# A third seven-product pair in the ninth up panel of each channel mixer

## The chip, the cores and the metric

The kernel runs on one core of one Trainium2 chip. The metric is the device time of one execution in microseconds (us). The core has five engines with queues of their own: TensorE does matrix products (PE in the profile; PEld is its loading of the stationary operand), VectorE (DVE) and ScalarE (ACT) do element-wise work, GpSimd (POOL) and SyncE (SP) here mostly issue transfers.

## The reference

The function is a decoder trunk of two layers on one sequence of 256 tokens, 2,048 wide, in fp32. Each layer is a mixer (gated linear attention in the first, forgetting attention in the second, both with heads that attend into 256 memory tokens) and then a channel mixer, and this document is about the channel mixer:

```python
def causal_dwconv(u, w, b):
    s_ = u.shape[1]
    up = jnp.pad(u, ((0, 0), (CONV_WIDTH - 1, 0), (0, 0)))
    return w[0] * up[:, 0:s_] + w[1] * up[:, 1:s_ + 1] + w[2] * up[:, 2:s_ + 2] + b

def conv_ffn(h, w_up, conv_w, conv_b, w_down):
    u = causal_dwconv(h @ w_up, conv_w, conv_b)
    a, val = split_cols(u, [FFN_HIDDEN, FFN_HIDDEN])
    return (jax.nn.silu(a) * val) @ w_down
```

`FFN_HIDDEN` is 5,632 and `h` is the normalized residual stream (256 x 2048). So `w_up` is 2,048 x 11,264 and `w_down` 5,632 x 2,048, in each layer.

## The kernel before

**Products in parts.** An fp32 operand is kept as two parts, a high part rounded to the format that TensorE takes (`whi`, written by ScalarE at line 231 or 380) and the low rest (`wlo`, VectorE, line 232 or 381). A product is three matmuls: high x high, low x high, high x low. Activations lie split in SBUF as `bufA` or `bufB` (the name in the profile is `A` or `B`, `mix` where the tile was given out again), one tile for each chunk of 128 channels. The weights come from DRAM (`wp`) and are split on the way.

**Panels.** The up projection is done in eleven panels (j = 0, 4, ..., 40; panel number j // 4, from 0). A panel has four blocks of results, two blocks of 128 tokens by two halves of 512 columns, each in a PSUM bank of its own, and runs over the 16 chunks of the 2,048 input channels. The order in a mixer is: up panels 0 to 4, the first part of the down projection (chunks 0 to 15, as two steps of 1,024 columns), up panels 5 to 7, the second part (chunks 16 to 27), up panels 8 to 10, the last part.

**One chunk, or two at once.** `pair_steps` (line 384) runs a panel. A chunk on its own takes `split_unit` (line 210): a 512 KB load to a tile `raw` (four rooms), one cast and one subtraction of 1,024 columns, and 12 matmuls of 512 columns. Two chunks k and k+1 can be taken together as a two-by-two block product with seven products (p1 to p7, with p2, p3 and p4 going to the banks of the blocks) in place of eight, so with 21 matmuls. That asks for sums and differences of the weights (VectorE, lines 435 to 438, in place in two 512 KB tiles `raw2`, of which there are two rooms, so one pair's), for four splits (`split_more`, line 375: one of 512 and three of 1,024 columns), for four banks more (p1, p5, p7, p6), and for sums and differences of the activations (`usum`, in the down projection `dsum`), which are made once by `input_sums` (line 1431) or `gated` (1415) through `token_sums` (468). `whi` and `wlo` have four rooms each; a pair uses all four. The results in p1, p5, p7 and p6 are added in by `early` (1486 for an up panel, 1334 for the down projection) after a panel's last pair.

**Which chunks are paired.** All up panels take chunks 6 and 7 as a pair (`SEVEN_UP`). Panels 5 and 8, those right after a part of the down projection, also take 11 and 12 (`SEVEN_MORE`, `MORE_IN`). In the down projection the pairs begin at chunks 4, 10, 20 and 34 (`SEVEN_DOWN`), with token sums in the rooms `dsum0` and `dsum1`. `pair_steps` puts a pair starting at chunk k where k chunks have been done; with `ahead` = 2, as in panels 5 and 8, two chunks earlier. The order there is 0, 1, 2, 3, 6-7, 4, 5, 8, 11-12, 9, 10, 13, 14, 15.

**The work beside the matmuls.** The results of a panel are turned on VectorE, moved through DRAM by POOL's queue, and come back 32-wide for the convolution (ScalarE, `tap_of`), two additions, silu and the gate (`gated`). These are put out in small steps: at each chunk `tick` (1465) is given a credit (1.45, or 1.7 in panels 5 and 8; 0 in the two ticks of a pair) and issues waiting steps while the credit is positive. Each step is tied behind the last split that was traced (`issue_after`). Splits, loads and pairs' differences have a higher priority by 300 instructions than the evacuations of banks. The final order on each engine is made by a planner from these priorities and from its own estimate of what is ready.

**Banks.** PSUM has four `acc` banks and four more, `ps_o`, two `ps_s` and `ps_t`. From one panel or down step to the next the two sets change places (`flip`): the blocks of one are in the set that takes p1, p5, p7 and p6 of the next.

Of the kernel before, what the change touches and what calls it, by code (L numbers as in the profile page):

```python
# [34 lines left out]
SEVEN_UP = (6,)  # L35
SEVEN_DOWN = {4: 0, 10: 1, 20: 0, 34: 1}
SEVEN_MORE = 11
MORE_IN = (5, 8)


LEVELS = (64, 16, 4)
# [77 lines left out]
def _layout():  # L119

    where, off = {}, 0
    for key, _, kcs, cols, per in _panels():
        n = sum(c[1] for c in cols)
        units = []
        for u in range(0, len(kcs), per):
            units.append((off, kcs[u : u + per], n))
            off += P * per * n
        where[key] = units
    return where, off
# [17 lines left out]
def _trunk(ctx: ExitStack, tc: tile.TileContext, xt, xtok, memt, wp, wgu, gns, gfin, cnv, par, msk, out):  # L147
    nc = tc.nc
    where, _ = _layout()
# [35 lines left out]
    loads, casts, lows, ends, last_mm, sent = [], [], [], [], [], []  # L185
# [282 lines left out]
    def token_sums(r, dst):  # L468

        t = r.rearrange("p s (b n) -> p (s b) n", b=2)  # L470
        a11, a21, a12, a22 = (t[:, n, :] for n in range(4))
        V.tensor_tensor(a22, a21, a22, ALU.add)
        V.tensor_tensor(a21, a11, a21, ALU.subtract)
        V.tensor_tensor(a11, a22, a11, ALU.subtract)
        V.tensor_tensor(a12, a12, a11, ALU.subtract)
        halves([dst[:, part] for part in range(2)], t)
# [903 lines left out]
    def ffn(l, nx, h, m, ys, zs, landing, then, pool, temps, last=None, spare=None):  # L1380
        with tc.tile_pool(name=f"ffn{l}", bufs=1) as fp:
            def held(name, i):
                return pool.tile([P, 2, 4, P], F32R, name=name, tag=f"{name}{i}")

            up_sums = {k: held("usum", k) for k in (*SEVEN_UP, SEVEN_MORE)}
# [45 lines left out]
            def input_sums(k):  # L1431

                r = fp.tile([P, 2, T], F32, name="cv", tag="cv")
                for s in range(2):
                    V.tensor_tensor(r[:, s, :], h[k + s][:, 0, :].bitcast(F32), h[k + s][:, 1, :].bitcast(F32), ALU.add)
                token_sums(r, up_sums[k])


            def scale(b):
                return nx.col()[:, b : b + 1]  # L1440

            def turn(j, wait):

                count[0] += 1
                slot = count[0] % 2
                y, z = ys[slot], zs[slot]

                def evac(b, a):
                    with tc.high_priority(offset=AHEAD):
                        turned_last[0] = V.transpose(y[:, :, :, b, :], a.rearrange("p (k c i) -> p c k i", c=4, i=32))  # L1450
                    if b:
                        away = far_away(dram, flat(y), T, nc.gpsimd)
                        back = lambda: away(flat(z))
                        steps = [(0.5, lambda s=s, c=c, i=i: tap_of(j, s, c, i, slot)) for n in ((1, 2), (0,))
                                 for s in range(2) for c in range(2) for i in n]
                        steps += [(1.0, lambda: add_tap(1)), (1.0, lambda: add_tap(2)), (0.5, silu),
                                  (1.0, lambda: gated(j, 0)), (0.7, lambda: gated(j, 1))]
                        returns.append((clock[0] + 3, slot, back, [(clock[0] + wait, *step) for step in steps]))

                return evac  # L1460

            waiting, clock, credit = [], [0], [0.0]
            returns, unread, turned_last = [], [0, 0], [None]

            def tick(share):

                clock[0] += 1
                credit[0] = min(credit[0], 0.0) + share
                while returns and returns[0][0] <= clock[0] and not unread[returns[0][1]]:
                    _, slot, back, steps = returns.pop(0)  # L1470
                    back()
                    unread[slot] = 12
                    waiting.extend(steps)
                while waiting and waiting[0][0] <= clock[0] and credit[0] > 0:
                    _, cost, step = waiting.pop(0)
                    credit[0] -= cost
                    step()

            def up_pair(j):

                count[2] += 1
                second = j // 4 in MORE_IN
                turns = [turn(j + 2 * h_, 7 if not h_ and j // 4 + 1 in MORE_IN else 8) for h_ in range(2)]
                u = {}

                def early(bank):
                    u.update({(b, h_): temps(2 * b + h_) for b in range(2) for h_ in range(2)})
                    S.activation(u[0, 1], bank["p1"], AF.Copy)
                    S.activation(u[0, 0], bank["p1"], AF.Copy, scale=scale(0))
                    V.tensor_tensor(u[0, 1], bank["p6"], u[0, 1], ALU.add)  # L1490
                    V.tensor_tensor(u[1, 0], bank["p7"], u[0, 1], ALU.add)
                    V.tensor_tensor(u[0, 1], bank["p5"], u[0, 1], ALU.add)
                    V.tensor_tensor(u[1, 1], bank["p5"], u[1, 0], ALU.add)
                    for b, h_ in ((0, 1), (1, 0), (1, 1)):
                        S.activation(u[b, h_], u[b, h_], AF.Copy, scale=scale(b))

                def late(b, h_, a):
                    with tc.issue_after(turned_last[0].ins) if h_ and not b else nullcontext():
                        V.scalar_tensor_tensor(u[b, h_], a, scale(b), u[b, h_], ALU.mult, ALU.add)
                    turns[h_](b, u[b, h_])  # L1500

                return pair_steps(where["up", l, j], h, {k: up_sums[k] for k in (*SEVEN_UP, SEVEN_MORE)[: 1 + second]},
                                  count[2] % 2, pool, early, late, 2 * second)

            def first(k):
# [3 lines left out]
                    input_sums(SEVEN_MORE)  # L1509
                tick(0)  # L1510

            def drive(steps, share=1.45):
                for k in steps:
                    tick(share if k >= 0 else 0.0)

            def drive_up(j):
                drive(up_pair(j), 1.7 if j // 4 in MORE_IN else 1.45)

            for k in SEVEN_UP:
                input_sums(k)  # L1520
            for k in up_pair(0):
                first(k)
            done = 4
            for p, (lo, hi) in enumerate(PARTS[:-1]):
                while done < hi + 4:
                    drive_up(done)
                    done += 4
                src = [m[c % RING] for c in range(lo, hi)]
                for f in (0, 2):
                    count[2] += 1  # L1530
                    drive(down_pair(l, p, f, src, {c - lo: t for c, t in sums.items() if f}, count[2] % 2, pool,
                                    lambda: (temps(0), temps(1))))
                sums.clear()
            lo, hi = PARTS[-1]
            while done < hi:
                drive_up(done)
                done += 4
# [86 lines left out]
    with tc.tile_pool(name="stash", bufs=1) as st:  # L1624
        vt = st.tile([P, 2, FOX_H * HD], F32, name="fvt")
        turned3 = vt.rearrange("p b t -> p (b t)").rearrange("p (f q k b j) -> p f q k b j", f=3, q=4, k=4, b=2)
        turned3 = [turned3[:, f] for f in range(3)]

        with tc.tile_pool(name="turn1", bufs=1) as tp:
            n2, then = preparing("kv", bufB, tp, dram, turned3, "raw2", nc.gpsimd)  # L1630
            ys = [const.tile([P, 4, 4, 2, 32], F32, name="yu", tag=tag) for tag in ("mk0", "mv0")]
            fixed = [vt.rearrange("p b t -> p (b t)")[:, 2048 + 512 * i : 2560 + 512 * i] for i in range(2)]

            def temps(i):
                return fixed[i] if i < 2 else tp.tile([P, 512], F32, name="temp", tag=f"temp{i}")

            more = []
            for t, tag in ((mk, "mk1"), (mv, "mv1")):
                parked.append(dram.tile([P, 4 * T], F32, name="park" + tag, tag="park" + tag, bufs=1))
                nc.gpsimd.dma_start(parked[-1], t[1].rearrange("p a b -> p (a b)"))  # L1640
                more.append(const.tile([P, 2, 2, T], F32R, name="more" + tag, tag=tag))
            ffn(0, n, bufB, bufA + [t[:, i] for t in more for i in range(2)], ys, turned3, ys, then, tp, temps)
        fox(n2, vt, turned3)
# [9 lines left out]
    with tc.tile_pool(name="store", bufs=1) as op:  # L1653
# [55 lines left out]
        then.begin, then.rooms = begin, None  # L1709
        more = [op.tile([P, 2, T], F32R, name=f"more{i}") for i in range(RING - KC)]  # L1710
        ffn(1, n, bufA, bufB + more, ys, zs, zs, then, op, temps, last, spare)


# [68 lines left out]
```

## Time and profile before

| | |
|---|---|
| median of 3 runs | 2213.76 us (2212.93 to 2215.54) |
| profiled execution | 2213.36 us, span of its instructions 2211.5 us |
| TensorE matmuls (PE) | 2200.9 us busy, 10,323 |
| VectorE (DVE) | 1784.5 us busy |
| ScalarE (ACT) | 1420.5 us busy |
| weight loads on SP's queue | 743 of 512 KB, 4.5 us from issue to landing |
| granted clock of TensorE | 0.998 |

All times within the profile are counted from the first instruction. Busy times are sums of rows; matmuls are pipelined, so that a row's 390 ns overlaps its neighbours, and the pace of the stream is read from the start times or from counts in a window. In lists of groups or timelines a row has the line in the kernel, the engine, the operation, what it writes and reads with shapes, how many there were, and in brackets idle time of the engine just before and what ended it.

### The profile page before, as it was taken

The page shows a single profiled execution, that of the slowest core. Times are in us where ns is not written, and L with a number is a line of the kernel's source. Part 1 is how long each engine was busy: PE and PEld are TensorE (multiplying, and loading weights), DVE is VectorE, ACT ScalarE, POOL GpSimd, SP SyncE. Part 2 cuts the span into 40 slices and gives each one's busy share as a digit, 9 for nine tenths or more (in the row PEclk, how much of TensorE's full clock was granted, in tenths as well). Part 3 has the DMA queues.
Part 4 walks back from the last instruction along what each step waited for, and adds up shares of the span by engine and source line. Part 5 has one row for each costly group of instructions (what it writes and reads, how often), then busy time and mean ns, then how long its engine had stood idle before and what let it go on. Part 6 is the DMA issues. An engine that isn't in the chain of part 4 may idle for free.

```text
span 2211.5 us, 30032 instructions
## 1 busy us (share of the span) xinstructions
PE 2200.9 (100%) x10323; PEld 1854.7 (84%) x10323; DVE 1784.5 (81%) x2640; ACT 1420.5 (64%) x2255; POOL 136.5 (6%) x257
## 2 busy tenths in 40 slices
PE   9999999999999999999999999999999999999998
PEld 7888888888888888888888998888888888888886
DVE  7768977688897878888978669668888788988896
ACT  6655664566787568656865555555788656764874
POOL 0000000001100000001110000000101000100000
PEclk9999999999999999999999999999999999999999
DMA  9767567767677567667677767677777757776674
GB/s 347 252 225 224 190 194 234 253 231 254 229 245 263 186 222 242 224 225 246 226 246 264 231 201 246 222 237 249 222 240 245 241 186 247 236 248 218 223 259 153
DMA packets 165713, 515.41 MB, mean 233 GB/s; under 512 B 20716, under 2 KB 41976, under 8 KB 165560
## 3 DMA queue, kind: packets, MB, share of 16 engines
q1 hardware_dynamic: 148488, 460.99, 62.9%
q0 software_dynamic: 16496, 51.71, 7.6%
q8 instruction: 81, 1.33, 0.2%
q10 hardware_dynamic: 576, 0.79, 0.1%
q14 instruction: 72, 0.59, 0.1%
HBM read 469.62 MB, written 43.79 MB: 232 GB/s over the span
## 4 chain that ended last, share of the span: by engine, by line
PE 99%; DMA 0%; DVE 0%; ACT 0%; SPq 0%; issue 0%; DVEq 0%
PE acc L410 30%; PE acc L336 26%; PE ps_s L410 15%; PE ps_o L410 8%; PE ps_t L410 7%; PE acc L307 3%; PE acc L262 3%; PE acc L366 2%; PE ps_s L336 2%; PE acc L260 1%; PE ps_s L1021 0%; PE ps_o L694 0%; DMA raw<-wp 0%; PE ps_s L694 0%; PE ps_s L1294 0%; PE ps_s L1067 0%
## 5 line engine op out<-in xcount | busy, mean ns | idle before, releaser
L232 DVE TENSOR_TENSOR wlo<-raw,whi 128x1024 fp32r<-128x1024 f32 (+2 forms) x707 | 845.4, 1204 | 236.1 <-ACT whi L231 216.6
L231 ACT ACTIVATE whi<-raw 128x1024 fp32r<-128x1024 f32 (+2 forms) x707 | 736.0, 1049 | 410.0 <-PE acc L336 130.5
L336 PE MATMUL acc<-whi,B 128*128 128x512 f32 (+3 forms) x1248 | 291.8, 370 | 0.0
L380 ACT ACTIVATE whi<-raw 128x1024 fp32r<-128x1024 f32 (+1 forms) x136 | 129.8, 954 | 188.9 <-PE acc L410 73.7
L336 PEld LDWEIGHTS acc<-whi,B 128*128 128x128 f32 x1248 | 226.9, 188 | 28.0
L381 DVE TENSOR_TENSOR wlo<-raw,whi 128x1024 fp32r<-128x1024 f32 (+1 forms) x136 | 147.8, 1089 | 59.6 <-ACT whi L380 56.6
L410 PE MATMUL acc<-whi,mix 128*128 128x512 f32 x764 | 194.7, 390 | 0.0
L410 PE MATMUL acc<-whi,B 128*128 128x512 f32 x750 | 192.6, 389 | 0.0
L410 PEld LDWEIGHTS acc<-whi,mix 128*128 128x128 f32 x764 | 143.5, 188 | 29.7
L410 PEld LDWEIGHTS acc<-whi,B 128*128 128x128 f32 x750 | 140.9, 188 | 29.1
L336 PE MATMUL acc<-wlo,B 128*128 128x512 f32 (+3 forms) x624 | 158.5, 369 | 0.0
L336 PEld LDWEIGHTS acc<-wlo,B 128*128 128x128 f32 x624 | 114.6, 188 | 14.6
L1400 ACT ACTIVATE tap<-fvt,cw 128x256 f32<-128x256 f32 x264 | 123.4, 530 | 1.2 <-DMA fvt<-far 1.1
L1400 ACT ACTIVATE tap<-yzu,cw 128x256 f32<-128x256 f32 x264 | 123.4, 531 | 0.4 <-DMA yzu<-far 0.2
L1407 DVE TENSOR_TENSOR tap<-tap,tap 128x1024 f32<-128x1024 f32 x88 | 107.1, 1217 | 1.1 <-ACT tap L1400 1.0
L410 PE MATMUL acc<-wlo,mix 128*128 128x512 f32 x382 | 107.4, 389 | 0.0
L410 PE MATMUL acc<-wlo,B 128*128 128x512 f32 x375 | 107.1, 390 | 0.0
L410 PE MATMUL ps_s<-whi,mix 128*128 128x512 f32 x386 | 105.9, 390 | 0.0
L410 PE MATMUL ps_s<-whi,B 128*128 128x512 f32 x342 | 93.3, 390 | 0.0
L410 PEld LDWEIGHTS ps_s<-whi,mix 128*128 128x128 f32 x386 | 72.5, 188 | 14.9
L410 PEld LDWEIGHTS acc<-wlo,mix 128*128 128x128 f32 x382 | 71.8, 188 | 14.8
L410 PEld LDWEIGHTS acc<-wlo,B 128*128 128x128 f32 x375 | 70.4, 188 | 14.6
(500 smaller groups left out, 3848.6 us busy)
## 6 DMA issues: line engine op xcount, KB each, us to landing
raw<-wp SPq DMA_DIRECT2D x743, 512.0 KB, 4.5
fvt<-far POOLq DMA_DIRECT2D x100, 128.0 KB, 5.6
raw<-wp SPq DMA_DIRECT2D x32, 384.0 KB, 3.5
far<-yu POOLq DMA_DIRECT2D x22, 512.0 KB, 5.8
far<-yzu POOLq DMA_DIRECT2D x22, 512.0 KB, 5.4
yzu<-far POOLq DMA_DIRECT2D x88, 128.0 KB, 5.3
raw<-wp SPq DMA_DIRECT2D x24, 388.0 KB, 4.2
x<-xtok SPq DMA_DIRECT2D x8, 512.0 KB, 7.2
```

Of the source, the lines that this page charges most:

```text
L231: casts.append(S.activation(hi[:, s], raw[:, s], AF.Copy))
L232: lows.append(V.tensor_tensor(lo[:, s], raw[:, s], hi[:, s].bitcast(F32), ALU.subtract))
L260: mm = TE.matmul(acc[p][c][:, :T], w[:, s], both[:, 0, :], start=False, stop=end and j == 3)
L262: mm = TE.matmul(acc[p][c], w[:, s], both, start=u == j == 0, stop=end and j == 3)
L307: mm = TE.matmul(acc[b][:, :n], src[kcs[j] - base][:, part, b * P : (b + 1) * P], w, start=u == 0 and low == part == j == 0, stop=u == end ...
L336: mm = TE.matmul(acc[b][:, :n], src[kc - base][:, part, b * P : (b + 1) * P], ready[low][:, j * room : j * room + n], start=i == low == pa ...
L366: mm = TE.matmul(acc[b][:, :n], src[kc - base][:, part, b * P : (b + 1) * P], w, start=i == low == part == j == 0, stop=i == end and low = ...
L380: casts.append(S.activation(hi[:, :n], src, AF.Copy))
L381: lows.append(V.tensor_tensor(lo[:, :n], src, hi[:, :n].bitcast(F32), ALU.subtract))
L410: r = TE.matmul(bank[name], x, w, start=name not in begun, stop=last)
L1400: S.activation(by_run(taps[i][:, s, c, i:]), zs[slot][:, :, 2 * c + s], AF.Copy if i else AF.Identity, bias=0.0 if i else w[3], scale=w[2 ...
L1407: V.tensor_tensor(taps[0], taps[0], taps[n][:, :, :, :T], ALU.add)
```

## The change

Panel 8 of each channel mixer takes chunks 3 and 4 as a third pair. The token sums for it are made in panel 6, behind its tenth step, into the room `dsum1`, which the down projection's chunk 10 has used and chunk 34 will use; three credits are taken off there. By the rule of `pair_steps` the order in panel 8 becomes 0, 3-4, 1, 6-7, 2, 5, 8, 11-12, 9, 10, 13, 14, 15.

```diff
+SEVEN_THIRD = 3
+THIRD_IN = 8
...
-                return pair_steps(where["up", l, j], h, {k: up_sums[k] for k in (*SEVEN_UP, SEVEN_MORE)[: 1 + second]},
+                keys = (*SEVEN_UP, SEVEN_MORE, SEVEN_THIRD)[: 1 + second + (j // 4 == THIRD_IN)]
+                return pair_steps(where["up", l, j], h, {k: up_sums[k] for k in keys},
                                   count[2] % 2, pool, early, late, 2 * second)
...
-            def drive(steps, share=1.45):
-                for k in steps:
+            def drive(steps, share=1.45, once=None):
+                for i, k in enumerate(steps):
                     tick(share if k >= 0 else 0.0)
+                    if i == 9 and once is not None:
+                        once()
+
+            def third_sums():
+                up_sums[SEVEN_THIRD] = held("dsum", 1)
+                with tc.issue_after(lows[-1].ins):
+                    input_sums(SEVEN_THIRD)
+                credit[0] -= 3.0
 
             def drive_up(j):
-                drive(up_pair(j), 1.7 if j // 4 in MORE_IN else 1.45)
+                drive(up_pair(j), 1.7 if j // 4 in MORE_IN else 1.45, third_sums if j // 4 == THIRD_IN - 2 else None)
```

## The prediction

> **What bounds the kernel now.** I read the page first: busy times, granted clock, the chain that ended last.
>
> ```profile
> span 2211.5 us, 30032 instructions
> PE 2200.9 (100%) x10323; PEld 1854.7 (84%) x10323; DVE 1784.5 (81%) x2640; ACT 1420.5 (64%) x2255; POOL 136.5 (6%) x257
> PEclk9999999999999999999999999999999999999999
> PE 99%; DMA 0%; DVE 0%; ACT 0%; SPq 0%; issue 0%; DVEq 0%
> ```
>
> TensorE is 99% of the chain, at full clock. Only two things can move the time: fewer matmuls, or a hole in their stream. So the next question is where the stream runs closest to what feeds it. For that I read the busy time by stage, with windows set on the ninth up panel (949.82 to 991.98), the tenth, the 21 us ahead of the ninth, the stretch behind its start, and the second half of the seventh panel; then, for the second mixer, the seventh and the 21 us ahead of the ninth.
>
> ```profile
> 949.82:991.98 42.16, 42.16 (x187) 34.94 (x186) 34.39 (x39) 22.75 (x25) 0.00 (x0) 1.00 0.58 198
> 991.98:1034.82 42.84, 42.84 (x190) 35.50 (x189) 34.17 (x40) 32.10 (x51) 5.50 (x10) 1.00 0.74 240
> 933.00:954.00 21.00, 21.00 (x94) 17.39 (x94) 20.63 (x26) 9.97 (x12) 0.00 (x0) 1.00 0.78 272
> 954.00:964.00 10.00, 10.00 (x46) 8.29 (x45) 8.23 (x10) 6.11 (x7) 0.00 (x0) 1.00 0.36 113
> 822.00:845.00 23.00, 23.00 (x103) 19.08 (x102) 20.95 (x28) 21.79 (x37) 0.00 (x0) 1.00 0.76 250
> ...
> 1860.00:1883.00 23.00, 23.00 (x103) 19.08 (x102) 20.93 (x27) 21.78 (x37) 0.00 (x0) 1.00 0.76 251
> 1971.00:1992.00 21.00, 21.00 (x94) 17.38 (x94) 20.74 (x26) 10.20 (x12) 0.00 (x0) 1.00 0.79 275
> ```
>
> Columns: window and its length, then busy time (and count) of PE, PEld, DVE, ACT and POOL, the clock, the DMA share, GB/s. Panel nine holds 186 weight loads in 42.16 us, panel ten 189 in 42.84: both 0.2267 us for each matmul (the 390 ns of a single row overlap with the next). Neither has a hole. But VectorE is busy 20.63 of the 21 us ahead of panel nine, 20.74 in the second mixer: it is full exactly where the change puts more on it.
>
> **The matmuls removed.** A chunk done alone costs 12 matmuls, two chunks 24; as seven products of three they cost 21. One pair more in panel nine of each of two mixers takes away 3 x 0.2267 = 0.68 us each, 1.36 us in all, 0.06%.
>
> **The order inside panel nine.** Today the order is chunks 0, 1, 2, 3, pair 6-7, then 4, 5, 8, pair 11-12, the rest. The third pair becomes second: 0, pair 3-4, 1, pair 6-7, 2, 5, 8, pair 11-12, then 9, 10, 13, 14, 15. So two pairs stand with a single chunk between them, right at the border to the down projection, whose sums VectorE is then still emptying. Pair 6-7 begins after 12 + 21 + 12 = 45 matmuls instead of 48: at 949.82 + 10.20 = 960.02 instead of 960.70.
>
> **What the pair adds to VectorE.** These are its instructions from the border through pair 6-7:
>
> ```profile
> 944.34 1.29 DVE L494 TENSOR_TENSOR x<-x,fvt 128x512 f32<-128x512 f32 x2
> 945.54 1.22 DVE L232 TENSOR_TENSOR wlo<-raw,whi 128x1024 fp32r<-128x1024 f32 x1
> ...
> 949.68 0.68 DVE L494 TENSOR_TENSOR x<-x,ps_o 128x512 f32<-128x512 f32 x1
> 950.28 0.68 DVE L494 TENSOR_TENSOR x<-x,ps_s 128x512 f32<-128x512 f32 x1
> 950.88 0.69 DVE L494 TENSOR_TENSOR x<-x,fvt 128x512 f32<-128x512 f32 x1
> 951.48 0.68 DVE L494 TENSOR_TENSOR x<-x,ps_t 128x512 f32<-128x512 f32 x1
> 952.08 1.22 DVE L232 TENSOR_TENSOR wlo<-raw,whi 128x1024 fp32r<-128x1024 f32 x1
> 953.21 0.68 DVE L494 TENSOR_TENSOR x<-x,ps_s 128x512 f32<-128x512 f32 x1
> 955.00 0.69 DVE L381 TENSOR_TENSOR wlo<-raw,whi 128x512 fp32r<-128x512 f32 x1 [1.10 <-ACT whi L380]
> 955.72 0.69 DVE L435 TENSOR_TENSOR raw<-raw 128x512 f32<-128x512 f32 x1
> 956.33 1.22 DVE L381 TENSOR_TENSOR wlo<-raw,whi 128x1024 fp32r<-128x1024 f32 x1
> 957.47 0.68 DVE L436 TENSOR_TENSOR raw<-raw,raw 128x512 f32<-128x512 f32 x1
> 958.19 0.69 DVE L437 TENSOR_TENSOR raw<-raw,raw 128x512 f32<-128x512 f32 x1
> 958.91 0.69 DVE L438 TENSOR_TENSOR raw<-raw 128x512 f32<-128x512 f32 x1
> 959.52 1.22 DVE L381 TENSOR_TENSOR wlo<-raw,whi 128x1024 fp32r<-128x1024 f32 x1
> 961.14 1.23 DVE L381 TENSOR_TENSOR wlo<-raw,whi 128x1024 fp32r<-128x1024 f32 x1 [0.40 <-ACT whi L380]
> ```
>
> Start to start, a 1,024-wide low half costs 1.14 us (956.33 to 957.47) and a 512-wide operation 0.60 to 0.72. A pair has three of the first and five of the second: 6.4 to 7.0 us. Ahead of pair 6-7 two single chunks (2.28) make room for it, so VectorE has 4.1 us more to do before that pair is ready. ScalarE gets 1.6 us more (3.5 casts of 1.06 for 2); it is busy 6.11 of the 10 us after 954, so it is not the bound.
>
> Its slack: the last low half of pair 6-7 is done at 961.14 + 1.23 = 962.37. TensorE needs it for the pair's 18th matmul, at 960.70 + 17 x 0.2267 = 964.55. That is 2.18 us of slack now; 0.68 of it goes because the pair starts earlier. Deficit: 4.1 + 0.68 - 2.18 = 2.6 us. The idle times in the rows, 1.10 and 0.40, can take 1.5 of it at best. From this side a hole of 1.1 to 2.6 us for each mixer.
>
> **The room of the raw weights.** Each pair loads two 512 KB tiles into two rooms, and the next pair's second load waits until the last low half of the pair before has read its tile. The rows for the issue and landing of pair 11-12, which waits like this today, and ScalarE's part:
>
> ```profile
> L429 SPq DMA_DIRECT2D raw<-wp x2: 328/328/328, 960.8 to 962.4; - x2
> DMA to landing us min/median/max: 3.2/3.4/3.6
> ```
> ```profile
> 949.84 1.07 ACT L231 ACTIVATE whi<-raw 128x1024 fp32r<-128x1024 f32 x1 [2.33 <-PE ps_t L410]
> 958.27 1.06 ACT L380 ACTIVATE whi<-raw 128x1024 fp32r<-128x1024 f32 x1 [2.19 <-DVE raw L436]
> ```
>
> 962.4 is indeed the end of pair 6-7's low halves. With the third pair, pair 6-7 waits for pair 3-4 in this way. The last low half of pair 3-4 writes over chunk 0's, whose matmuls end at 949.82 + 12 x 0.2267 = 952.54; with 0.25 for the signal and 1.22 of work it ends at 954.0 at the earliest. Then the load, 3.4; ScalarE, 1.06; a low half, 1.14; three differences, 2.0; a low half, 1.22: 962.8. TensorE needs that one for the pair's 12th matmul, at 960.02 + 11 x 0.2267 = 962.5. So 0.3 us is missing even if nothing else stands in the way. But by 953.89 VectorE is without a gap today, and the pair's 6.4 for the 3.4 us of chunks 1 to 3 puts 3.0 more into this row: if the low half waits for all of it, it ends at 956.9 and 3.2 us is missing. Hole by this chain: 0.3 to 3.2.
>
> **The accumulators.** The pair's products p1, p5, p7 and p6 go to the banks which the rows above empty (ps_o, ps_s, ps_s, ps_t, the last done at 953.89). Today they are first written at 960.70; then at 952.54, 954.58, 955.26 and 955.94. Slack is 1.4 us on the tightest (955.26 against 953.89). The 3.0 us more on VectorE can fall ahead of these or ahead of the weights, not wholly on both: 0 to 1.6 us here. The three bounds describe the same 3 us on one engine, so I do not add them: 0 to 3.2, and I take the middle of the second chain, 1.8 us for each mixer, which lies inside the first one's 1.1 to 2.6. If evacuation and load chain do add, 3.2 + 1.6 = 4.8.
>
> **The token sums** move into panel seven: two 256-wide and four 128-wide additions, one ScalarE copy and one low half:
>
> ```profile
> L1435 DVE TENSOR_TENSOR cv<-B x4: 412/419/424, 451.4 to 486.5; 128x256 f32<-128x256 f32 x4
> L472 DVE TENSOR_TENSOR cv<-cv x12: 276/283/291, 453.6 to 2090.3; 128x128 f32<-128x128 f32 x12
> L680 ACT ACTIVATE usum<-cv x4: 616/628/633, 462.4 to 1530.7; 128x512 fp32r<-128x512 f32 x4
> L681 DVE TENSOR_TENSOR usum<-cv,usum x4: 683/689/694, 463.1 to 1532.0; 128x512 fp32r<-128x512 f32 x4
> ```
>
> 2 x 0.42 + 4 x 0.28 + 0.69 = 2.7 us of VectorE and 0.63 of ScalarE, where VectorE has 23 - 20.95 = 2.05 idle (2.07 in the second mixer). The credit of 3.0 taken at the same place holds the convolution work back by two steps. I take nothing on the path; without that cover 0.6 us for each mixer. Counting the steps, the work held back is still behind by two when the down projection ends, so its last step falls on the last chunk before panel nine: the additions move inside the full 21 us, they do not leave it. SP issues the same number of loads of the same size (pair 3-4 as two 512 KB tiles, its rooms free since the down projection's pair); POOL gets nothing. Pair 11-12 begins at 949.82 + 102 x 0.2267 = 972.94 and its rooms come free with pair 6-7's last low half, at about 964 to 966, so 7 to 9 us ahead against 11 now (962.4 to 973.62). The chain above needs 3.4 + 1.06 + 1.14 + 2.0 + 1.22 = 8.8 up to a product that starts 2.5 us into the pair: nothing taken, up to 0.5 us if the later end of both holds.
>
> **Sum.** 2 x (1.8 - 0.68) = +2.2 us. The profiled execution took 2213.36 us, 1.9 around its span of 2211.5, so 2215.6; the median of the runs shown, 2213.76, lies 0.4 higher, so 2216.0. What a measurement can tell from no change here is about 0.2%, 4.4 us.
>
> **The rivals.** (1) No hole: the planner lets the evacuations and differences fall into the idle 1.5 us, and chunk 1 stands in for the rest. Then the full 1.36 us is gained: 2212.4. For it: panel nine has two pairs and no hole today. Against it: 0.3 us missing even in the best chain. 0.20. (2) The hole of 0.3 to 2.8 us, as summed: 2213 to 2218. 0.35. (3) Slower beyond 0.2%: VectorE becomes the bound at the border, late with banks and weights in turn, and gaps add instead of overlapping. The point from which this decides is a hole of 2.9 us for each mixer, as 2 x (2.9 - 0.68) = 4.4; at 4.8 it gives +8.2, 2222. For it: 20.63 of 21 busy and 3.0 us put in. 0.36. (4) The hole is one piece of over 3 us and the clock drops. The start of this kernel shows a slow array:
>
> ```profile
> 1.46 4.21 PE L183 MATMUL ps_o<-B 128*128 128x512 f32 x9 [1.46 <-DVE B L180]
> ```
>
> Nine matmuls of 512 take 4.21 us, some 0.43 each, against 0.2267. Nine at that pace lose 9 x 0.20 = 1.8 us behind each hole: with holes of 4.8, 2222 + 3.6 = 2226. 0.06. [...]
>
> **Chances.** Faster 0.03; same 0.20 + 0.35 = 0.55; slower 0.36 + 0.06 = 0.42. The likeliest single time is that of (2) and its own range is 2213 to 2218; the range with four in five reaches from (1) into (3): 2212 to 2223.
>
> **What would show it.** Step one: 183 matmuls in panel nine. Step two: weight rows of L381 for pair 3-4 near 945 to 956, and evacuations of L494 pushed past 954. Step three: idle time of TensorE between 952 and 964, put down to DVE wlo or a DVE evacuation, 1 to 3 us in each mixer, and panel nine at 41.5 + 1.8 = 43.3 us. I am wrong if panel nine takes 41.5 (rival 1), if its hole exceeds 2.9, or if time comes from another stage, the seventh panel above all.

## The result and the profile after

The changed kernel takes 2223.8 us (median of six runs, 2221.39 to 2225.11) against 2213.49 for the kernel before, a ratio of 1.0046 with a 95% interval of 1.0035 to 1.0057: 10.3 us slower. The profiled execution, 2225.11 us, is the slowest of the six; the mean granted clock is 0.997 in the three slowest and 0.999 in the fastest, so the two slow stretches described below need not occur in every execution. The first lines of the page after:

```profile
span 2223.3 us, 30066 instructions
PE 2205.3 (99%) x10317; PEld 1853.2 (83%) x10317; DVE 1796.1 (81%) x2666; ACT 1423.7 (64%) x2261; POOL 136.6 (6%) x257
PE 96%; DVE 2%; DMA 1%; ACT 1%; issue 0%; SPq 0%; ACTq 0%; DVEq 0%
```

The six matmuls are gone (10,317), and yet TensorE's share of the chain fell from 99% to 96%: some of the chain now runs through VectorE, ScalarE and a load. The windows below hold panel nine of both mixers, and two stretches inside the first (columns as before):

```profile
949.97:997.70 47.73, 44.19 (x184) 34.90 (x183) 38.70 (x46) 24.36 (x27) 0.00 (x0) 0.96 0.50 171
968.10:969.60 1.50, 1.50 (x6) 1.09 (x7) 1.50 (x2) 1.50 (x2) 0.00 (x0) 0.96 0.35 139
969.60:973.00 3.40, 3.40 (x10) 2.70 (x9) 3.40 (x4) 1.75 (x3) 0.00 (x0) 0.52 0.71 212
1994.32:2042.06 47.74, 44.31 (x184) 34.78 (x183) 38.69 (x46) 24.34 (x27) 0.00 (x0) 0.96 0.52 174
```

Panel nine took 42.16 us and now takes 47.73, with three matmuls fewer: two times 5.57 us, 11.1 of the 11.8 by which the span grew. TensorE stands for 3.5 us in it by the busy times, and for 3.4 us from 969.60 on the granted clock is 0.52. Six matmuls of panel nine now run at 946.34 already, ahead of the down projection's last sixteen. The window therefore begins at 949.97, where TensorE has done as many matmuls as before panel nine began at 949.82 in the kernel before; it holds as many as the panel has (183 by the weight loads), and next to nothing was lost ahead of it. The timeline of TensorE has the places where it stood, called holes from here on:

```profile
957.32 0.74 PE L412 MATMUL ps_t<-whi,dsum 128*128 128x512 f32 x2 [1.04 <-ACT whi L382]
963.15 0.72 PE L412 MATMUL acc<-whi,B 128*128 128x512 f32 x2 [0.73 <-ACT whi L382]
968.04 0.73 PE L412 MATMUL ps_t<-whi,usum 128*128 128x512 f32 x2 [1.77 <-ACT whi L382]
```

The first is product p6 of pair 3-4 (`dsum`, in the bank `ps_t`), waiting for the cast of the fourth split. The second is p2 of pair 6-7, waiting for the second cast, the third p6 of pair 6-7, again for the fourth. Taken from one matmul's start to the next, less 0.227, the holes are 1.21, 0.89 and 1.93 us; a further 0.1 goes at the next step behind each. The second mixer has the same three (1.21, 0.80, 1.94). The chain that ended last, between 950.09 and 968.04, says why (start, length, what):

```profile
950.09 0.60 DVE x L496
950.69 0.34 DVE mix L527
951.02 0.60 DVE raw L438
951.62 0.34 DVE mix L527
951.96 1.79 DVE x L496 x3
953.75 0.60 DVE raw L439
...
955.41 0.69 DVE raw L440
...
956.21 1.07 ACT whi L382
...
957.29 1.24 DVE wlo L383
...
958.55 3.38 DMA raw<-wp
...
962.03 1.07 ACT whi L382
...
964.27 1.22 DVE wlo L383
965.49 0.61 DVE raw L439
...
966.12 0.70 DVE raw L440
...
966.93 1.06 ACT whi L382
...
968.04 0.73 PE ps_t L412 x2
```

The differences of pair 3-4 (L438 to L440) stand in VectorE's queue between evacuations of the down projection (L496) and the last of the convolution work (L527). So the fourth cast is late, the first hole. With it the last low half is late (957.29), and only when that is done may the second tile of pair 6-7 be loaded (958.55). The second hole is the wait for its landing, and behind the landing come, one after the other, cast, low half, differences and cast: the third hole. From the end of the fourth cast of pair 3-4 (957.27) to p6 of pair 6-7 (968.04) this chain takes 10.8 us.

### The profile page after: what moved, and what is told of

It reads as the page before. It is cut to its first block, busy times and chain, and to the rows that moved or that the text cites. A ratio compares the mean times of both kernels' runs of the same rounds, so it can differ in the third digit from the quotient of the medians.

```text
span 2223.3 us, 30066 instructions
## 1 busy us (share of the span) xinstructions
PE 2205.3 (99%) x10317; PEld 1853.2 (83%) x10317; DVE 1796.1 (81%) x2666; ACT 1423.7 (64%) x2261; POOL 136.6 (6%) x257
## 4 chain that ended last, share of the span: by engine, by line
PE 96%; DVE 2%; DMA 1%; ACT 1%; issue 0%; SPq 0%; ACTq 0%; DVEq 0%
PE acc L412 28%; PE acc L338 26%; PE ps_s L412 15%; PE ps_o L412 7%; PE ps_t L412 7%; PE acc L309 3%; PE acc L264 3%; PE acc L368 2%; PE ps_s L338 2%; PE acc L262 1%; DMA raw<-wp 1%; DVE wlo L383 0%; PE ps_s L1023 0%; ACT whi L382 0%; DVE x L496 0%
## 5 line engine op out<-in xcount | busy, mean ns | idle before, releaser
L382 ACT ACTIVATE whi<-raw 128x1024 fp32r<-128x1024 f32 (+1 forms) x144 | 137.1, 954 | 211.3 <-PE ps_t L412 70.6
L383 DVE TENSOR_TENSOR wlo<-raw,whi 128x1024 fp32r<-128x1024 f32 (+1 forms) x144 | 156.2, 1088 | 63.6 <-ACT whi L382 60.1
```

The costliest lines, as they stand in the source:

```text
L382: casts.append(S.activation(hi[:, :n], src, AF.Copy))
L383: lows.append(V.tensor_tensor(lo[:, :n], src, hi[:, :n].bitcast(F32), ALU.subtract))
```

## The experiments

Four accounts were open: the token sums and the work held back for them; VectorE's queue at the border to the down projection; the two rooms of the pairs' raw weights; and the clock. In the diffs, minus stands for the changed kernel.

**The sums without the pair.**

```diff
-                keys = (*SEVEN_UP, SEVEN_MORE, SEVEN_THIRD)[: 1 + second + (j // 4 == THIRD_IN)]
+                keys = (*SEVEN_UP, SEVEN_MORE, SEVEN_THIRD)[: 1 + second]
```

> The token sums are made in panel seven and the three credits taken, but panel nine keeps its two pairs, so the sums are not used. Theory (the holes in panel nine are the whole loss): no hole appears, 2213.5 us, within 1 us of before. Rival (the sums and the work held back cost on their own): 0.6 us or more for each mixer, up to 2216.

2213.12 us against 2213.00, ratio 1.0000 (0.9991 to 1.0009). The sums and the work held back cost nothing that shows.

**The credits not taken.**

```diff
-                credit[0] -= 3.0
```

> The changed kernel without the three credits taken at the token sums, so the convolution work is not held back and nothing of it is left for the last two chunks before panel nine (two additions and a gate, some 2.5 us of VectorE there). Theory (VectorE's queue at the border makes the first hole, 1.2 us at p6 of pair 3-4): the first hole goes and the rest shrinks by about the same, 2 x 1.5 us or more off 2223.8, about 2219 to 2221 or less if the slow clock goes too. Rival (only the order of the pairs counts): no change, 2223 to 2224.

2222.1 us against 2213.24, ratio 1.0040 (1.0027 to 1.0054). The first hole went from 1.21 to 1.05 us only, and the third stayed 1.93; the second is 0.79 us in the first mixer and 1.21 in the second. So the convolution work that was moved to the border is not what crowds it; the theory's figure for this run, two times 1.5 us, was not met. The time lies 1.7 us below the changed kernel's. In the profiled run the holes add up to about the same, but one of the two slow stretches (1.6 us) is missing, with the same hole ahead of it: windows of the first and the second mixer behind the third hole.

```profile
966.90:970.40 3.50, 3.50 (x16) 2.75 (x17) 3.50 (x4) 3.16 (x4) 0.00 (x0) 1.00 0.51 183
2009.60:2013.00 3.40, 3.40 (x9) 2.58 (x9) 3.40 (x4) 2.57 (x4) 0.00 (x0) 0.51 0.46 169
```

**Less work on VectorE ahead of panel nine.** Four additions to the residual stream are left out of the second part of the down projection (its second step), so the output lacks them; `some_add` adds nothing.

```diff
         def early(bank):
             t0, t1 = temps()
             S.activation(t0, bank["p1"], AF.Copy)
+            add_to = some_add if (p, f) == (1, 2) else every_add
             add_to(f)(0, t0)
...
-            add_to(f + 1)(1, bank["p5"])
+            every_add(f + 1)(1, bank["p5"])
```

> The changed kernel with four of the additions to the residual stream left out in the second down projection's second step (those of the pair's results p1, p6 and p7), so its output is not the reference's; 2.4 us of VectorE less in the 20 us ahead of panel nine. Theory: the first hole (1.2 us) goes, the load of pair 6-7 is issued 1 us or more earlier, and the third hole falls under the size that sends the clock down: 2214 to 2218. Rival (the hole comes of the chain of waits between the engines, not of the amount of work): still 2221 or more.

2218.83 us against 2213.24, ratio 1.0025 (1.0016 to 1.0034), 0.8 above the range that the theory gave. The first hole is gone in both mixers, so with less work at the border it does not arise; the second shrank to 0.07 and 0.40 us. But the third is unchanged, the only one listed in the first mixer. The fourth cast of pair 3-4, from ScalarE's timeline, and the third hole:

```profile
953.95 1.06 ACT L382 ACTIVATE whi<-raw 128x1024 fp32r<-128x1024 f32 x1 [3.04 <-DVE raw L440]
...
965.55 0.73 PE L412 MATMUL ps_t<-whi,usum 128*128 128x512 f32 x2 [1.77 <-ACT whi L382]
```

That cast ends at 955.01, and p6 of pair 6-7 comes 10.5 us later, against 10.8 in the changed kernel. So the chain from this cast over the room and the load to p6 is nearly as long without the border's work, and the third hole is not the border's.

**Other rooms for pair 3-4.**

```diff
-                    ra, rb = [pool.tile([P, NUNIT], F32, name="raw2", tag="raw2", bufs=2) for _ in range(2)]
+                    ra, rb = [rear.tile([P, NUNIT], F32, name="raw", tag="raw", bufs=4) if k == SEVEN_THIRD else
+                              pool.tile([P, NUNIT], F32, name="raw2", tag="raw2", bufs=2) for _ in range(2)]
```

> The changed kernel, but pair 3-4 loads its weights into two of the four rooms of the single chunks, so that pair 6-7's second load need not wait for pair 3-4's last low half. Theory of the rooms: the first hole of panel nine (1.2 us at p6 of pair 3-4) stays, the second (0.9 us, waiting for the load) goes and the third (1.9 us) with the slow clock behind it shrinks below 1 us: 2 x (1.3 to 2.2 - 0.68) over before, 2214.7 to 2216.5 us. Rival (VectorE alone): its queue is no shorter, the third hole stays above 1.5 us with its slow stretch, 2220 us or more.

2216.73 us against 2213.00, ratio 1.0017 (1.0008 to 1.0026), 0.2 above the theory's range. SP's queue issues both tiles of pair 6-7 at 944, where the changed kernel's second went at 958.55:

```profile
944.11 0.90 SPq L432 DMA_DIRECT2D raw<-wp  x2
```
```profile
957.07 0.74 PE L412 MATMUL ps_t<-whi,dsum 128*128 128x512 f32 x2 [1.04 <-ACT whi L382]
963.71 1.20 PE L412 MATMUL ps_s<-whi,usum 128*128 128x512 f32 x4 [0.18 <-ACT whi L382]
965.16 0.74 PE L412 MATMUL ps_t<-whi,usum 128*128 128x512 f32 x2 [0.25 <-ACT whi L382]
```

As TensorE's timeline shows, the first hole stays, the second is gone, the third is 0.34 + 0.42 us in two pieces, and the clock does not drop (mean granted clock 0.999). The rooms are the second and most of the third hole.

**Both at once.** Again the output lacks those four additions.

> Both single cures at once in the changed kernel: pair 3-4 loads into rooms of the single chunks, and four additions to the residual stream are left out ahead of panel nine (the output is not the reference's). Theory (the holes are the vector queue at the border, and the rooms, and nothing else): no hole over 0.3 us in panel nine, no slow clock, 0.8 to 1.4 us less than before, 2211.9 to 2212.6. Rival (something third keeps TensorE waiting, such as the order of the differences): 2214 or more, as with the rooms alone less the first hole.

2212.67 us against 2213.00, ratio 0.9999 (0.9989 to 1.0008). Holes of some 0.2 us are left, with the steps behind them 0.9 us over both mixers by the starts of the matmuls; 1.36 less 0.9 gives 0.5 below before, and 0.3 was measured, which the interval does not tell from nothing. Border and rooms together account for the holes.

**The low half behind the differences.** In the changed kernel's pair 6-7 the low half at 964.27 ran ahead of the two differences that the fourth cast needs. The edit puts it behind them in all three pairs of panel nine.

```diff
-                w3 = split_more(ra, 1024)
+                w3 = split_more(ra, 1024, ready if SEVEN_THIRD in sums else None)   # low half behind the last difference
```

> The changed kernel with the low half of the third split tied behind the pair's last two differences on VectorE, in panel nine alone. In the changed kernel that low half (1.14 us) ran ahead of them in pair 6-7, and the fourth cast, which p6 waits for, had to wait for both. Theory: the third hole shrinks from 1.93 to about 0.8 us and the clock no longer drops: 2 x (1.1 + 1.5) off 2223.8, 2218.6, or, if p5 then waits for its low half instead, 2221. Rival (the load's landing alone sets the third hole): 2223 or more.

2220.73 us against 2213.00, ratio 1.0034 (1.0021 to 1.0047). TensorE's timeline has

```profile
956.18 0.74 PE L413 MATMUL ps_t<-whi,dsum 128*128 128x512 f32 x2 [0.51 <-ACT whi L382]
962.98 0.73 PE L413 MATMUL acc<-whi,B 128*128 128x512 f32 x2 [1.25 <-ACT whi L382]
966.86 0.73 PE L413 MATMUL ps_t<-whi,usum 128*128 128x512 f32 x2 [1.26 <-ACT whi L382]
```

The first and third hole shrank to 0.67 and 1.42 us (1.17 in the second mixer), so the order on VectorE makes about half of the first hole too. But the second grew to 1.41, because p2 came to its wait earlier and the load landed at 961.76 in place of 961.93; the second mixer has 1.20 there and a fourth hole of 0.59 at p1 of pair 6-7. The holes of both mixers add up to nearly what they did, 8.3 us against 8.8, though no slow stretch is left (mean granted clock 0.999): the 3.1 us gained are about the two slow stretches. So the theory was right in the clock and wrong in the sum of the holes; the landing of the load holds the end of the chain.

**The third hole filled.** Eight more matmuls on the low parts, ahead of p6 of pair 6-7 in panel nine; each adds the small product low x low to p7.

```diff
+                if fill and k == fill[0]:
+                    for _ in range(fill[1]):
+                        mm("p7", st[2][1], w3[1][:, 512:], False)
                 three("p6", st[1], [t[:, 512:] for t in w4], done)
```

> The changed kernel with eight more matmuls of 512 columns between p7 and p6 of pair 6-7 in panel nine, each adding the low x low product to p7 (a term some 2 to the 24th smaller, harmless): 1.81 us of work where TensorE stood for 1.94. If the third hole is what sends the clock down, the eight matmuls at 0.43 us go back to 0.227, 1.6 us for each mixer: 2220.5 us. If the slow clock comes of the other holes or of something else, the time stays at 2223.8; if the matmuls only add, 2227.

2221.07 us against 2213.00, ratio 1.0037 (1.0023 to 1.0050), 2.7 below the changed kernel with 16 matmuls more. No slow stretch is left, and the mean granted clock is 0.999 in all five executions; the window behind p6:

```profile
968.00:971.50 3.50, 3.50 (x17) 2.78 (x16) 3.50 (x4) 2.66 (x4) 0.00 (x0) 1.00 0.53 181
```

Without the hole the clock stays up, 1.00 in this window against 0.52 behind the hole of the changed kernel: the slow stretch is the hole's consequence, and by its eight matmuls at 0.427 in place of 0.227 us it is 1.6 us of each mixer's loss.

**Longer holes.** In the kernel before, the cast of chunk 12 is repeated in eight up panels of each mixer.

```diff
-                casts.append(S.activation(hi[:, s], raw[:, s], AF.Copy))
+                for _ in range(1 + again):
+                    casts.append(S.activation(hi[:, s], raw[:, s], AF.Copy))
```

> The kernel before, with the cast of chunk 12 done over 8 to 12 times more in each up panel but the first, sixth and ninth, so that TensorE stands before that chunk for a length that grows with the count, from none to some 3 us, 16 places in two mixers. It shows the clock behind single holes. [...]

2451.45 us, one run. The holes came out at 9.3 to 15.3 us, far over the none to 3 that were asked for, so this run says nothing about short ones; each of the 16 is followed by 8 to 12 matmuls at 0.43 us. With fewer repetitions:

> As the run with the repeated casts, but 2 to 5 more casts in place of 8 to 12, whose holes came out at 9 to 15 us. By the slope of that run, about 1.5 us for each repetition, the holes should be 0 to 5 us. [...]

2336.96 us, one run. The holes are 2.8 to 7.7 us, again longer than planned. All from 3.87 up are followed by 5 to 13 slow matmuls. The two at the short end, the same place in the two mixers, fell out differently. TensorE's timeline at the first and at the second:

```profile
535.06 0.73 PE L412 MATMUL ps_o<-whi,B 128*128 128x512 f32 x2 [2.61 <-ACT whi L233]
...
1636.16 0.74 PE L412 MATMUL ps_o<-whi,A 128*128 128x512 f32 x2 [2.62 <-ACT whi L233]
```

and the windows behind the second and the first (clock in the third column from the end):

```profile
1636.20:1641.00 4.80, 4.80 (x21) 3.95 (x22) 4.80 (x5) 0.10 (x1) 0.00 (x0) 1.00 0.48 147
...
536.10:539.40 3.30, 3.30 (x9) 2.62 (x8) 3.30 (x4) 0.00 (x0) 0.00 (x0) 0.50 0.60 212
```

**The pairs spread.** Sums and pairs as in the change; the order in panel nine is given by hand.

```diff
+SPREAD = [0, 1, 2, 5, 6, 8, 9, 11, 10, 13, 3, 14, 15]
...
+        plan = order or plan
```

> Same three pairs, same sums, but the order in panel nine is 0, 1, 2, 5, pair 6-7, 8, 9, pair 11-12, 10, 13, pair 3-4, 14, 15: two single chunks between pairs, four ahead of the first. Theory (place next to the border and next to each other makes the holes): no hole, 186 - 3 matmuls, 1.36 us less than before, 2212.1 us. Rival (a third pair is too much for VectorE or for the two rooms wherever it stands): holes of about 1 us or more for each mixer, 2214 us or more.

2211.81 us against 2213.00, ratio 0.9994 (0.9986 to 1.0003). Panel nine has no hole. One of 0.76 us is left 24 us into panel ten of the second mixer (not at its start, as the next expectation says), where ScalarE's queue stood behind a transfer of the convolution's input; another of 0.80 us, at 1163.17, lies outside the channel mixers. ScalarE's row:

```profile
2049.80 1.31 ACT L1404 ACTIVATE tap<-yzu,cw 128x256 f32<-128x256 f32 x3 [3.10 <-DMA yzu<-far]
```

With `SPREAD = [0, 1, 2, 6, 5, 8, 11, 9, 10, 3, 13, 14, 15]`:

> Order in panel nine 0, 1, 2, pair 6-7, 5, 8, pair 11-12, 9, 10, pair 3-4, 13, 14, 15: as in the spread order, but with three single chunks ahead of the first pair and three behind the last, so that the last pair's results are taken up before the panel ends. Theory: the one hole of 0.76 us that the spread order left at the start of panel ten of the second mixer goes, none comes at the border: 1.36 us below before, 2211.6. Rival (three chunks are too few at the border): holes of about 0.5 us or more for each mixer, 2212.6 or more.

2211.75 us against 2213.24, ratio 0.9994 (0.9985 to 1.0003). Panel nine in both mixers:

```profile
949.53:991.01 41.48, 41.48 (x185) 34.37 (x183) 36.83 (x45) 22.24 (x24) 0.00 (x0) 1.00 0.52 180
1986.87:2028.46 41.59, 41.59 (x185) 34.20 (x183) 35.76 (x43) 22.24 (x24) 0.00 (x0) 1.00 0.51 177
```

41.48 us is 183 times 0.2267: no hole, with the three pairs in the panel. The panel is 0.68 and 0.57 us shorter than before, and the median lies lower by 1.2 to 1.5 in the two spread orders; the interval just takes in no change, so the gain is shown by the trace and not by the times.

**A second pair in every other up panel too,** on top of the last order: `second = j > 0`, order 0, 1, 2, 3, 6-7, 4, 5, 8, 9, 11-12, 10, 13, 14, 15, credit 1.7.

> The early spread order in panel nine, and pair 11-12 also in the eight up panels that had one pair, in the order 0, 1, 2, 3, 6-7, 4, 5, 8, 9, 11-12, 10, 13, 14, 15, with a credit of 1.7 in all of them. If spread pairs cost no hole anywhere, 16 more pairs take 16 x 0.68 = 10.9 us off 2211.8: 2201. Rival (VectorE, 34.2 of 42.8 us busy in panel ten, cannot take 4.1 us more beside the convolution, or the evacuations are late at the panels' ends): holes eat the gain, 2208 or more.

2266.14 us against 2213.00, ratio 1.0231 (1.0214 to 1.0248). The rival's forecast held, and far beyond what it gave. Holes of 0.5 to 2.9 us stand at the pairs in most of these panels, and seven slow stretches behind them; TensorE's timeline at one hole:

```profile
556.94 1.20 PE L415 MATMUL ps_s<-whi,usum 128*128 128x512 f32 x4 [1.51 <-ACT whi L384]
```

By the starts of the matmuls, holes of over 0.23 us add up to 48 us (0.4 in the run with the early spread order), the slow stretches to 12 more than there, the steps behind holes to 6 more; less the 10.9 us of matmuls taken away, this is 55 of the 56 us by which the span is longer than that run's. So the loss lies in these holes. What makes each of them late, VectorE beside the convolution, the evacuations or the credit of 1.7, was not traced.

## Why the prediction was wrong

It gave 2216.0 us, 2212 to 2223, and the likeliest case within 0.2%; measured is 2223.8, slower beyond that.

*Matmuls removed, 0.68 us for each mixer:* right. 10,317 are left, and a panel nine without holes takes 41.48 us.

*The order inside the panel:* right, 0, 3-4, 1, 6-7, by the rows. With the same pairs in another order nothing is lost.

*VectorE full at the border; the room of the raw weights:* both mechanisms were at work. The chain of the second, load, cast, low half, differences, ran as written, 3.38 us for the landing against 3.4. But the first was worked out for pair 6-7 alone, and the first hole stands at pair 3-4 itself.

*"The three bounds describe the same 3 us on one engine, so I do not add them":* this is the step that failed. They add, because they bite one after the other. The border delays the fourth cast of pair 3-4, and p6 waits for it, 1.32 us with the step behind it; no term of the sum has this wait. The room's chain then starts from that same cast, and the landing of its load holds up pair 6-7 twice (1.0 and 2.1). That is 4.4 us where I took 1.8: the room's chain measured 3.1, inside its 0.3 to 3.2 but 1.3 above the middle that I took, and the 1.32 is missing altogether. The removal runs show the parts: less work takes out the first hole and leaves the third, other rooms take out the second and most of the third and leave the first, and both together leave 0.9 us over the two mixers.

*The room's chain, 0.3 us at best:* too small. With the border's work taken out, the second and third hole with their steps are still 2.1 us in the first mixer and 2.5 in the second. At best I let the last low half of pair 3-4 end at 954.0, as soon as it had a room to write to; in that run it still had to wait for its own cast, which ends at 955.01, and the load went out at 956.29. The 0.25 for the signal is in the trace before: the low half at 965.27, released by the last matmul on `ps_s`, starts 0.26 us behind the start of the next matmul, at 965.01. And in my chain the last link was the low half for p5; on the chip it was the fourth cast for p6, behind a low half that had been put ahead of the differences.

*The accumulators, 0 to 1.6 us:* no matmul in panel nine of either mixer waited for a bank, so 0: TensorE's waits there, 3.5 and 3.4 us, are all for ScalarE's casts. VectorE's added work went ahead of the weights: the last of the evacuations ends at 953.75, against 953.89 before.

*The clock, as a rival with 0.06 and only with a hole of over 3 us in one piece:* the second part of the failure. No run stood behind the 3 us. It needed no such hole; 1.93 us was followed by the slow stretch in both mixers, eight matmuls x 0.2 = 1.6 us each. Holes and clock give 4.4 + 1.6 - 0.68 = 5.3 us for each mixer, 10.6 in all, against the 11.1 by which the two panels grew in the profiled execution and the 10.3 between the medians.

*The sums at no cost:* right, 2213.12 against 2213.00. *Work held back stays inside the full 21 us:* right; giving it back took 0.16 us off the first hole.

Rival 3, slower with gaps that add, came nearest: +8.2 at holes of 4.8 us, without the clock. Its 4.8 lies near the 4.4 in part by luck: 1.6 of it was for banks, which cost nothing.

## What to carry to other kernels

A stage in which the bound engine never waits can have its slack used up by a change that takes work off that engine; ask of each helper's chain how much it is ahead, and when the wait for one late item is followed by a chain that starts from the same item, add the two rather than take the larger. In panel nine place decided: three pairs cost 10.3 us with one single chunk between the first two at a stage border, and nothing with three or more ahead of the first and two or more between them, so it pays to space the heavy steps before giving them up. The runs do not tell how much the distance from the border does and how much the spacing. Nor is spacing enough everywhere: with four single chunks between the pairs, a second pair in eight other panels of each mixer, with more credit, came out 53 us slower. A hole in TensorE's stream costs more than its own length when the clock follows it down (1.6 us more behind each hole of 1.93 us in the changed kernel), and filling it with idle matmuls can be cheaper than leaving it (2221.07 us against 2223.8).

## What the runs showed of the hardware

Behind a hole of 1.93 us in the matmul stream the granted clock was about half over the next 3.4 us in some places and full in others. Of the six third holes of 1.93 or 1.94 us, four were followed by a clock of 0.50 to 0.52 (both mixers of the changed kernel, and the second mixer with the credits not taken and with less work on VectorE) and two by 1.00 (the first mixer in those two runs). In the runs with repeated casts, of the two of 2.8 us one was followed by 0.50 and one by 1.00; all of 16 between 9.3 and 15.3 us were followed by slow matmuls, and all 14 between 3.87 and 7.7 us. The run with more pairs has more of them: behind holes of 2.17 and 2.89 us and one of two of 1.92 the clock fell, behind 1.51, 2.62 and the other of 1.92 it did not. No hole of 1.51 us or less that stood alone was followed by a fall in any run; one of 1.68 us with one of 0.42 close behind it was (0.52 from 558.60 to 562.00 in that run). What decides between equal holes, and how long a lone hole must be for the clock to fall, was not measured: the runs made for it gave longer holes than were asked for.
